# Key norms by one product with a block matrix of ones, and the steps of recurrence, inversion and finish in another order

## The chip, the cores and the metric

The kernel runs on one core of a Trainium2 chip, in one launch. The metric is the device time of one execution in microseconds (us). Six names recur: PE is TensorE (matrix products; its weight loads are shown apart as PEld), DVE is VectorE, ACT is ScalarE, POOL is GpSimd, SP is the engine that issues most transfers, and PSUM is the memory into which PE writes.

## The reference, cut to what matters

One hybrid decoder layer for 512 tokens of width 1024, in float32. A normalised stream feeds two mixers, RWKV-7 time mixing (16 heads of 64 channels) and a native sparse attention; their outputs are gated, merged, projected, and followed by a gated MLP with a short convolution. What the change touches is in the time mixing:

```python
r, k, v, wd, ad, gd = split_cols(z, RWKV_SPLIT)
decay = jnp.exp(-jnp.exp(w_log.astype(f32)))
a = jax.nn.sigmoid(a0 + ad @ a2)
g = jax.nn.sigmoid(gd) @ g2
kk = heads(k * k_k)
kk = kk / jnp.maximum(jnp.sqrt(jnp.sum(kk * kk, axis=-1, keepdims=True)), 1e-12)
k = k * (1.0 + (a - 1.0) * k_a)
# state = state * w + (state a) b^T + v k^T, token by token; y = state r
y = wkv7_scan(r_h, heads(decay), k_h, v_h, -kk, kk * a_h)
mean = jnp.mean(y, axis=-1, keepdims=True)
var = jnp.mean(jnp.square(y - mean), axis=-1, keepdims=True)
y = ((y - mean) * lax.rsqrt(var + GN_EPS)).reshape(B, S, RWKV_DIM)
y = y * ln_w + ln_b
y = (y + bonus.reshape(B, S, RWKV_DIM)) * g
```

and, at the end of the layer, `x = x + rms_norm(... @ ffn_down)`, whose sum of squares and root stand behind the last product.

## The kernel before, in words

**Wide products.** Each large weight matrix is cut in blocks of 128 columns. A block is split into a rounded part (named with h) by ScalarE and the rest (l) by GpSimd, and multiplied with the stream's parts in groups of three PE instructions of 128x512 (L306, L307, L308; the same three in other lines for the later projections). These triples are called wide products below; `k`, `r`, `v` (time mixing), `gt` (gates), `q`, `ksp`, `kwp` (attention) are their results.

**Who sets the order.** The program is written as generators. A function `drive(fill, ...)` goes in rounds: in each round every spawned generator advances by its own rate (0.6 steps, 1.05 steps, and so on, after a delay in rounds), and `fill`, a chain of projections, advances by one step, which is one triple. So a `yield` in a generator leaves room for a triple or two on PE at that place; more yields mean more wide products there, taken from the same chain. A scheduler then places the instructions on each engine's queue, mostly in the order in which they were written. Every engine works through its queue in order.

**Stages.** The 16 heads are 8 pairs (p = 0 to 7) in two groups (g = 0, 1) of four pairs (GP = 4). For each pair `prep` makes decays, key norms and scaled keys, and `couple` the products within chunks of 64 tokens, with the projections of the next pair as fill. For each group `invert` inverts 32x32 triangular blocks on DVE, `recur` joins them to 64x64 inverses on PE and then goes through 8 chunks of 64 tokens, and `finish` normalises the output and multiplies it with the output gate. In the run shown the first group's recurrence lies at 225 to 282 us, the second's at 437 to 488; then comes the attention's score stage (`pc` compressed scores, `s` scores of a head for 128 queries, `vtp`, `pt`, `pct` transposes, `o` values), with the rest of the query and key projections as fill, and from about 700 us the output projections and the MLP.

**The places the change touches.** Line numbers are those of the profile.

- `prep`. Q is the square of the scaled key, made by ACT. Four products `pn` (L541) of Q with `sel`, a 128x2 matrix that selects the two heads, give token norms in a 128x8 tile; ACT takes the root (L543, after a load of its table), DVE a maximum and a reciprocal (L544, L545), POOL spreads the result to 128x512 (L551, `nte`; ACT for pair 4), and four transposes (`pb`, L140 with `ident`) bring it back to channels by tokens. `EC` and `EN` are exponentials of the summed log decay `C` (a scan on DVE, L531) and its negative. `A` (L561, L562) needs `EN`, Q (L563) needs `EC`; `KB` (L570) and `AR` (L572) multiply with `pb`. `couple` multiplies `KB` and `AR` in the products `g` (L607).
- `recur`, joining: `mt` (L705) are 64 products of 32x32 per group in two halves (q) of two pairs (i); each half is evicted by ACT and DVE, then four yields, then `mm` (L728), 64 more, evicted into `TT` (L733 on ACT, L735 on DVE), then three yields.
- `recur`, the chunks: for chunk c, `xw` (L789) multiplies the state, DVE adds to W, 8 products with `TT` (L805) give U, which ACT and DVE evict into `UV` (L810 on ACT); a yield; `xs` (L815) are the products that renew the state; a yield. The output `y` is gathered in two PSUM banks for four chunks: `carried(c)` from the state (L753), `inner(c)` from `UV` (L760); every second chunk is copied to `YT` (L764). `inner(c - 1)` stands behind `xw` of chunk c.
- `finish`, for each pair: load and split of the gate weights (`gh` on ACT, `gl` on POOL; the copy at L854), load of the bonus `bvl`, transposes `gt`, scale and shift on ACT into `y2`, addition of `bvl` on POOL, the product `pg` (L880) and the multiplication on DVE (L881). `finish` of group 1 is spawned ahead of the scores at rate FN.
- `post`: at the end of each block of tokens ACT gives a sum of squares (L1361), DVE a product `p2tm` (L1363) and the total `p2ss` (L1364); ACT takes the root, DVE the reciprocal (L180) and two final steps (L1368).

## Time and profile before

| | |
|---|---|
| median of 3 runs | 1170.33 us (1169.43 to 1172.22) |
| the profiled execution | 1171.52 us |
| its span on the core | 1169.7 us |
| mean granted PE clock | 0.992 |
| instructions in the span | 19903 |
| DMA | 131.95 MB, mean 113 GB/s |

The span is the time from the first to the last instruction that the profiler saw; the execution's own time is 1.8 us more. A row of a timeline has start and duration; "xN" is a count of pieces that stand together (an fp32 product shows as two pieces), and in square brackets stands how long the engine had been idle and what released it. Since matmuls overlap, the durations of neighbours on PE add up to more than the time they take: the distance of starts is the time. A row of the waits has the engine and instruction that waited, who released it, the total, the number of times and the longest. A row of the windows has, for a stretch of time, the busy time and number of instructions of each engine, and the TensorE clock that was granted as a share of full speed.

### The profile page before, as it was taken

To read this page: it belongs to the slowest core of one execution; us is meant where nothing else is said; L and a number is where in the kernel's file an instruction comes from. 1 tells how busy PE (TensorE), PEld (TensorE's weight loads), DVE (VectorE), ACT (ScalarE), POOL (GpSimd) and SP (SyncE) were. 2 spreads that over 40 slices of the span, in tenths; PEclk is the share of its full clock that TensorE was granted. 3 is DMA by queue.
4 is the path that set the end of the run, shared out by engine and by line. 5 is a ranking of instruction groups with operands and counts; after the bars stand their busy time and mean duration, and the time that the engine had idled before them with its cause. 6 is when DMAs were issued, how large, how long until landed. Compare 5 with 4: busy or idle time off the path is not lost.

```text
span 1169.7 us, 19903 instructions
## 1 busy us (share of the span) xinstructions
PE 1148.6 (98%) x7418; PEld 927.3 (79%) x7418; DVE 574.0 (49%) x1196; ACT 579.5 (50%) x1149; POOL 595.2 (51%) x537
## 2 busy tenths in 40 slices
PE   9999999999999999999999999999999999999997
PEld 7888888867878887767677778889888888888886
DVE  4236555634456563587798735754443343331103
ACT  6446663534665334477576654534444444443311
POOL 4346654335666452497666635511565556554430
PEclk9999999989999999999999999999999999999999
DMA  7522335311443662225543136641233333334421
GB/s 245 134 65 75 103 99 167 96 64 53 113 125 93 188 198 92 91 60 145 170 149 97 46 97 181 209 156 39 80 99 99 97 94 99 99 97 136 127 64 72
DMA packets 95651, 131.95 MB, mean 113 GB/s; under 512 B 34177, under 2 KB 37057, under 8 KB 95298
## 3 DMA queue, kind: packets, MB, share of 16 engines
q1 hardware_dynamic: 79634, 116.26, 33.1%
q10 hardware_dynamic: 15920, 14.42, 3.9%
q8 instruction: 58, 0.95, 0.3%
q14 instruction: 39, 0.32, 0.1%
HBM read 108.30 MB, written 19.14 MB: 109 GB/s over the span
## 4 chain that ended last, share of the span: by engine, by line
PE 87%; DVE 4%; ACT 3%; POOL 2%; issue 1%; DMA 1%; SPq 0%; DVEq 0%; ACTq 0%; POOLq 0%
PE pu L223 6%; PE pu L221 6%; PE pu L222 6%; PE dn L1317 3%; PE dn L1316 3%; PE dn L1315 3%; PE o L1142 3%; PE pt L140 3%; PE ub L1199 3%; PE ub L1201 2%; PE ub L1200 2%; PE gt L306 2%; PE gt L308 2%; PE gt L307 2%; PE v L306 2%; PE v L308 2%
## 5 line engine op out<-in xcount | busy, mean ns | idle before, releaser
L1095 ACT ACTIVATE p<-p,stt 128x384 f32<-128x384 f32 (+3 forms) x128 | 70.7, 554 | 34.5 <-DVE stt L1093 32.9
L1069 POOL TENSOR_SCALAR p<-p,stt 128x512 f32<-128x512 f32 (+1 forms) x64 | 72.3, 1139 | 25.8 <-DVE stt L1064 15.5
L1457 DVE SCALAR_TENSOR_TENSOR u<-pu,cvec,u 128x511 f32<-128x511 f32 x44 | 33.0, 750 | 101.2 <-ACT u L1456 101.2
L1093 DVE CUSTOM_DVE_ANT_0 p<-s,rh 128x384 f32<-128x384 f32 (+3 forms) x128 | 59.0, 484 | 22.7 <-PE s L1079 18.3
L1463 DVE TENSOR_TENSOR al<-u,ah 128x512 fp32r<-128x512 f32 x22 | 23.8, 1080 | 45.4 <-ACT ah L1462 45.4
L140 PE MATMUL pt<-ident,p 128*128 128x128 f32 x320 | 44.3, 272 | 0.0
L1086 PE MATMUL s<-kst,qs 128*128 128x512 f32 (+1 forms) x128 | 39.2, 396 | 4.4 <-DVE stt L1093 4.1
L1461 POOL TENSOR_TENSOR u<-u,u 128x512 f32<-128x512 f32 x22 | 28.3, 1288 | 27.3 <-DVE u L1458 26.3
L1142 PE MATMUL o<-PT,vt 128*64 128x256 f32 (+3 forms) x256 | 41.5, 443 | 0.0
L140 PEld LDWEIGHTS pt<-ident,p 128*128 128x128 f32 x320 | 37.8, 141 | 4.4 <-issue 0.4
L1069 DVE TENSOR_SCALAR p<-p,stt 128x512 f32<-128x512 f32 (+1 forms) x64 | 35.3, 580 | 0.8
L1456 ACT ACTIVATE u<-pu,cvec 128x512 f32<-128x512 f32 x44 | 33.6, 764 | 3.0 <-PE pu L1419 3.0
L1458 DVE SCALAR_TENSOR_TENSOR u<-pu,cvec,u 128x510 f32<-128x510 f32 x44 | 33.0, 749 | 1.6
L1086 PEld LDWEIGHTS s<-kst,qs 128*128 128x128 f32 x128 | 20.9, 189 | 13.5 <-DVE stt L1093 9.3
L1142 PEld LDWEIGHTS o<-PT,vt 128*64 128x64 f32 x256 | 16.6, 136 | 18.8 <-issue 16.8
L1133 ACT ACTIVATE PT<-pt 128x512 f32<-128x512 f32 x48 | 27.3, 584 | 8.0 <-PE pt L140 7.8
L1363 DVE TENSOR_TENSOR p2tm<-dn,gb 128x512 f32<-128x512 f32 x4 | 2.8, 692 | 51.2 <-ACT p2jl L1361 51.2
L1135 DVE COPY PT<-pt 128x512 f32<-128x512 f32 x32 | 21.7, 678 | 8.4 <-PE pt L140 8.3
L1462 ACT ACTIVATE ah<-u 128x512 fp32r<-128x512 f32 x22 | 13.9, 633 | 22.0 <-POOL u L1461 22.0
L1095 ACT ACTIVATION_READ_ACCUMULATOR p<-p,stt 128x1 f32 x128 | 24.2, 189 | 0.0
L664 DVE TENSOR_TENSOR XP<-XP,TM 128x30 f32<-128x30 f32 (+14 forms) x60 | 20.3, 338 | 2.0
L162 POOL TENSOR_TENSOR up3l<-up30r,up3h 128x512 fp32r<-128x512 f32 x1 | 1.3, 1295 | 38.2 <-ACT up3h L124 38.2
(1755 smaller groups left out, 3953.8 us busy)
## 6 DMA issues: line engine op xcount, KB each, us to landing
gtd<-gt ACTq DMA_DIRECT2D x16, 256.0 KB, 2.2
qs<-qd SPq DMA_DIRECT2D x32, 128.0 KB, 3.3
g<-gtd SPq DMA_DIRECT2D x16, 256.0 KB, 3.2
xt<-in_x_dram SPq DMA_DIRECT2D x4, 512.0 KB, 5.5
bvd<-bv SPq DMA_DIRECT2D x8, 256.0 KB, 2.2
bvl<-bvd SPq DMA_DIRECT2D x8, 256.0 KB, 2.9
oad<-y SPq DMA_DIRECT2D x8, 256.0 KB, 2.5
kst<-kst ACTq DMA_DIRECT2D x16, 128.0 KB, 2.5
```

What stands on the lines that cost most here:

```text
L140: return te.transpose(o, i, ident)
L221: te.matmul(p, wh(k), mh(k), start=first and k == 0, stop=False)
L222: te.matmul(p, wh(k), ml(k), start=False, stop=False)
L223: te.matmul(p, wl(k), mh(k), start=False, stop=last and k == n - 1)
L306: te.matmul(p, wh(k), hh[:, k, :], start=k == 0, stop=False)
L308: te.matmul(p, wl(k), hh[:, k, :], start=False, stop=k == KT - 1)
L1069: (po if b else ve).tensor_scalar(o.pe[e, b, k], o.pe[e, b, k], st[e][:, 3, i:i + 1], None, op0=OP.mult)
L1086: m = te.matmul(s_[:, :n], qt, kt[:, x, b, :n], start=x == 0, stop=x == 1)
L1093: ve.tensor_tensor_reduce(sb, parts[b], rh[e][:, (3 - qb) * 128:], -1.0, BIG, OP.add, OP.min, st[e][:, 0, i:i + 1])
L1095: sc.activation(sb, sb, AF.Exp, scale=-1.0, bias=st[e][:, 0, i:i + 1], accum_out=st[e][:, 1, i:i + 1])
L1142: te.matmul(acc[e * 64:e * 64 + 64, j * 128:], vt[:, j, b * 256 + g * 64:b * 256 + g * 64 + 64], m[e][:, c:c + n], start=False, stop=k == ...
L1199: te.matmul(p, wh(k), sh[:, k, :], start=k == 0, stop=False)
```

## The change

1. **Key norms.** The 128x128 matrix `onesr`, with ones in the two 64x64 blocks of a head, multiplies Q in one fp32 product: `pb` in PSUM holds the sum of squares of the head in every one of its channels. DVE raises it to at least 1e-24, ACT takes the logarithm and then exp(-0.5 ...) in place. The factors 2 and -2 become 0.5 and -1, so the first use of `pb` becomes a scalar_tensor_tensor. `sel` goes.
2. **Joining the inverses.** After each quarter (q, i) of `mt` and of `mm` there are two yields; the four yields and the three yields behind them become one each.
3. **Chunks.** `inner(c)` stands at the end of its own chunk, behind `xs`; `carried(c)` is always ahead of W, for c = 4 too; the two `y` banks are taken when c is a multiple of 4.
4. **Finish.** The gate weights are loaded and split in place of a helper, with the rest part cut to what is used; the shift `lnb` goes into the DVE multiplication. In group 0 DVE adds the scaled transposes to `bvl` in place (no ACT step, no POOL addition; two `bvl` buffers in turn), in group 1 ACT scales and POOL adds as before, with one yield more. FN becomes 1.3.
5. **post.** `p2ss` stands ahead of `p2tm`.

The diff, without the constants `sel`:

```diff
--- before.py
+++ after.py
@@ -34,3 +34,3 @@
 PR, CR, IY, FR = 0.6, 0.5, 31, 0.5
-ID, IE, RD, RR, NG0, NQ1, PX, FN = (30, 30), (54, 54), (67, 67), (1.05, 0.85), 8, 4, 3, 1.15
+ID, IE, RD, RR, NG0, NQ1, PX, FN = (30, 30), (54, 54), (67, 67), (1.05, 0.85), 8, 4, 3, 1.3
 NW, NU, PA = 13, 3, 0.25
@@ -538,15 +537,7 @@
         yield
-        pn = (pz if p == GP else py)(f"pn{p}")
-        for t in range(4):
-            te.matmul(pn[:, 2 * t:2 * t + 2], Q[:, t * 128:(t + 1) * 128], sel, start=True, stop=True)
-        nt = rw.tile([128, 8], F32, tag="nt", name=f"nt{p}", bufs=2)
-        sc.activation(nt, pn[:, :8], AF.Sqrt)
-        ve.tensor_scalar(nt, nt, 1e-12, 2.0, op0=OP.max, op1=OP.mult)
-        ve.reciprocal(nt, nt)
-        nte = rw.tile([128, 8, 64], F32, tag="T", name=f"nte{p}", bufs=NT)
-        nb = nt[:, :, None].to_broadcast([128, 8, 64])
-        if p == GP:
-            sc.activation(nte, nb, AF.Copy)
-        else:
-            po.tensor_copy(nte, nb)
+        pb = pz(f"pb{p}")
+        te.matmul(pb, onesr.bitcast(F32), Q, start=True, stop=True)
+        ve.tensor_scalar(pb, pb, 1e-24, None, op0=OP.max)
+        sc.activation(pb, pb, AF.Ln)
+        sc.activation(pb, pb, AF.Exp, scale=-0.5)
         EC = rw.tile([128, 8, 65], F32, tag="EC", name=f"EC{p}", bufs=1)
@@ -566,8 +557,6 @@
         yield
-        pb = pz(f"pb{p}")
-        for t in range(4):
-            tr(pb[:, t * 128:(t + 1) * 128], nte[:, 2 * t:2 * t + 2].rearrange("p a b -> p (a b)"), ident)
-        ve.tensor_tensor(KB[:, :, 0, :], pb.rearrange(c8, t=64), A.rearrange(c8, t=64), op=OP.mult)
+        ve.scalar_tensor_tensor(KB[:, :, 0, :], pb.rearrange(c8, t=64), 0.5, A.rearrange(c8, t=64), op0=OP.mult,
+                                op1=OP.mult)
         o.Q = None if gr else Q
-        ve.scalar_tensor_tensor(gr.AR[p % GP][:, 0, :] if gr else Q, Q, -2.0, pb, op0=OP.mult, op1=OP.mult)
+        ve.scalar_tensor_tensor(gr.AR[p % GP][:, 0, :] if gr else Q, Q, -1.0, pb, op0=OP.mult, op1=OP.mult)
         tc.keep_in_program_order(ve.scalar_tensor_tensor(F, R, vec[:, V_RK + p:V_RK + p + 1], F, op0=OP.mult,
@@ -708,2 +697,4 @@
                             tc.keep_in_program_order(m)
+                yield
+                yield
             for h in range(2):
@@ -718,4 +709,3 @@
             behind(sc.activation(gr.diag[0][lo, :, 0:32], gr.diag[1][lo], AF.Copy))
-        for _ in range(4):
-            yield
+        yield
         for q in range(GP // 2):
@@ -729,2 +719,4 @@
                                   stop=True)
+                yield
+                yield
             for h in range(2):
@@ -736,7 +728,6 @@
         YT = gr.YT = rh_.tile([128, 4, GP, 2, 64], F32, tag="XB", name=f"YT{g}", bufs=2)
-        for _ in range(3):
-            yield
+        yield
         hs = [slice(0, 64), slice(64, 128)]
         iv = "p (i v) -> p i v"
-        yps = {}
+        yps = [None]
 
@@ -745,5 +736,5 @@
         def ybank(c):
-            if c // 4 not in yps:
-                yps[c // 4] = [py(f"y{g}{c}{h}").rearrange("p (a i v) -> p a i v", i=GP, v=64) for h in range(2)]
-            return [b[:, c // 2 % 2] for b in yps[c // 4]]
+            if c % 4 == 0:
+                yps[0] = [py(f"y{g}{c}{h}").rearrange("p (a i v) -> p a i v", i=GP, v=64) for h in range(2)]
+            return [b[:, c // 2 % 2] for b in yps[0]]
 
@@ -756,3 +747,3 @@
         def inner(c):
-            y = ybank(c)
+            y = ybank(c) if c == 0 else [b[:, c // 2 % 2] for b in yps[0]]
             for h in range(2):
@@ -790,3 +781,2 @@
                                   St[hs[h], i], start=True, stop=True)
-                inner(c - 1)
                 if c != 4:
@@ -823,5 +813,5 @@
                 St = SN
+            inner(c)
+            if c < 7:
                 yield
-            else:
-                inner(c)
         stat2(2, free)
@@ -851,7 +841,11 @@
             gh = rh_.tile([128, 256], F32R, tag="gh", name=f"gh{p}", bufs=1)
-            gl = rh_.tile([128, 256], F32R, tag="gl", name=f"gl{p}", bufs=1)
-            split_to(a["g2"][p], gh, gl, f"g2{p}", 256, p=rh_, late=True, tag="TM", bufs=1)
-            po.tensor_copy(gh[64:96, 128:], gl[64:96, 128:].bitcast(F32))
+            gl = rh_.tile([128, 128], F32R, tag="gl", name=f"gl{p}", bufs=1)
+            raw = rh_.tile([128, 256], F32, tag="TM", name=f"g2{p}r", bufs=1)
+            sy.dma_start(raw, a["g2"][p])
+            tc.keep_in_program_order(sc.activation(gh, raw, AF.Copy))
+            po.tensor_tensor(gl, raw[:, :128], gh[:, :128].bitcast(F32), op=OP.subtract)
+            gx = gh[64:96, 128:]
+            po.tensor_tensor(gx, raw[64:96, 128:], gx.bitcast(F32), op=OP.subtract)
             yield
-            bvl = rh_.tile([128, S], F32, tag="bvl", name=f"bvl{p}", bufs=1)
+            bvl = rh_.tile([128, S], F32, tag=("bvl", "TB")[g == 0 and i % 2], name=f"bvl{p}", bufs=1)
             tc.keep_in_program_order(sy.dma_start(bvl, bvd[p]))
@@ -862,3 +856,3 @@
                 tr(pt[:, t * 128:(t + 1) * 128], Y8[:, t].rearrange("p h v -> p (h v)"), ident)
-            y2 = rh_.tile([128, S], F32, tag="TB", name=f"y2{p}", bufs=1)
+            y2 = bvl if g == 0 else rh_.tile([128, S], F32, tag="TB", name=f"y2{p}", bufs=1)
             y2v = y2.rearrange("p (t s u) -> p t s u", s=2, u=64)
@@ -866,8 +860,9 @@
             lnw, lnb = vec[:, V_LNW + p:V_LNW + p + 1], vec[:, V_LNB + p:V_LNB + p + 1]
-            if i % 2 == 0:
-                sc.activation(y2, pt, AF.Identity, scale=lnw, bias=lnb)
-            else:
-                for x in range(2):
-                    sc.activation(y2v[:, :, x], ptv[:, :, 1 - x], AF.Identity, scale=lnw, bias=lnb)
-            po.tensor_tensor(y2, y2, bvl, op=OP.add)
+            for y_, p_ in ([(y2, pt)] if i % 2 == 0 else [(y2v[:, :, x], ptv[:, :, 1 - x]) for x in range(2)]):
+                if g:
+                    sc.activation(y_, p_, AF.Copy, scale=lnw)
+                else:
+                    ve.scalar_tensor_tensor(y_, p_, lnw, y_, op0=OP.mult, op1=OP.add)
+            if g:
+                po.tensor_tensor(y2, y2, bvl, op=OP.add)
             yield
@@ -875,2 +870,3 @@
                 yield
+                yield
             pg = px(f"pg{p}")
@@ -878,5 +874,5 @@
             te.matmul(pg, gh[:, :128], lg1l, start=False, stop=False)
-            te.matmul(pg, gl[:, :128], lg1h, start=False, stop=False)
+            te.matmul(pg, gl, lg1h, start=False, stop=False)
             te.matmul(pg, gh[:96, 128:], lg2, start=False, stop=True)
-            ve.tensor_tensor(y2, y2, pg, op=OP.mult)
+            ve.scalar_tensor_tensor(y2, y2, lnb, pg, op0=OP.add, op1=OP.mult)
             sy.dma_start(oad[p], y2)
@@ -1362,4 +1358,4 @@
         tm = p.tile([128, 512], F32, tag=name + "tm", name=f"{name}tm{t}", bufs=3)
-        ve.tensor_tensor(tm, acc, gb[:, 512:], op=OP.mult)
         ve.tensor_tensor(ss[:, 2:3], ss[:, 0:1], ss[:, 1:2], op=OP.add)
+        ve.tensor_tensor(tm, acc, gb[:, 512:], op=OP.mult)
         r = rstd_of(ss[:, 2:3], D, f"{name}r{t}", p)
```

What it does to the order on an engine, at three places. First PE at the start of the first group's joining (`gt`, L306 to L308, is fill); before:

```order
L308 MATMUL gt_2323<-hh,gt04l_2325 128x512
L541 MATMUL pn_2345<-sel,Q_2301 128x2 x4
L306 MATMUL gt_2323<-hh,gt04h_2324 128x512
L307 MATMUL gt_2323<-hl,gt04h_2324 128x512
L308 MATMUL gt_2323<-hh,gt04l_2325 128x512
L705 MATMUL mt_2365<-x_2126 32x32 x32
L705 MATMUL mt_2400<-x_2126 32x32 x32
L306 MATMUL gt_2323<-hh,gt04h_2330 128x512
```

and now (L694 is the line of `mt` in the changed kernel):

```order
L308 MATMUL gt_2277<-hh,gt04l_2279 128x512
L694 MATMUL mt_2313<-x_2080 32x32 x16
L306 MATMUL gt_2277<-hh,gt04h_2284 128x512
L307 MATMUL gt_2277<-hl,gt04h_2284 128x512
L308 MATMUL gt_2277<-hh,gt04l_2285 128x512
L306 MATMUL gt_2277<-hh,gt04h_2284 128x512
L307 MATMUL gt_2277<-hl,gt04h_2284 128x512
L308 MATMUL gt_2277<-hh,gt04l_2285 128x512
L694 MATMUL mt_2313<-x_2080 32x32 x16
L306 MATMUL gt_2277<-hh,gt04h_2284 128x512
```

A row of `mt` with x32 or x16 is that many products of 32x32. All 64 stood together, and `pn` of pair 4 stood three rows ahead; now there are four pieces of 16 with six wide products between them, and `pn` is gone. `mm` is cut in the same way. Counted over the first group's joining and chunks the wide products rise from 63 to 95 and the blocks of small products from 22 to 31; over the second's from 74 to 97 and from 23 to 32.

Second PE in the score stage, at the first head pairs (L1079 and L1086 before, L1075 and L1082 now, are `s`); before:

```order
L307 MATMUL ksp_5461<-hl,ksp1h_5462 128x512
L1079 MATMUL s_5442<-kst_4161,qs_4884 128x512 x2
L308 MATMUL ksp_5461<-hh,ksp1l_5463 128x512
L306 MATMUL ksp_5461<-hh,ksp1h_5462 128x512
L307 MATMUL ksp_5461<-hl,ksp1h_5462 128x512
L308 MATMUL ksp_5461<-hh,ksp1l_5463 128x512
L1079 MATMUL s_5484<-kst_4161,qs_4884 128x256 x2
L306 MATMUL ksp_5461<-hh,ksp1h_5462 128x512
L307 MATMUL ksp_5461<-hl,ksp1h_5462 128x512
```

and now:

```order
L1075 MATMUL s_5344<-kst_4063,qs_4667 128x512 x2
L1075 MATMUL s_5386<-kst_4063,qs_4667 128x256 x2
L140 MATMUL pt_5457<-ident,p_5265 128x128
L140 MATMUL pt_5457<-ident,p_5228 128x128
L140 MATMUL pt_5457<-ident,p_5268 128x128
L140 MATMUL pt_5457<-ident,p_5231 128x128
L140 MATMUL pct_5448<-ident,sc_5209 64x128
L1075 MATMUL s_5403<-kst_4063,qs_4670 128x512 x2
L140 MATMUL pct_5448<-ident,sc_5209 64x128 x2
L1075 MATMUL s_5422<-kst_4063,qs_4670 128x256 x2
```

The wide products `ksp` stood between the scores; now 16 of them stand inside the second recurrence, and at this place scores and transposes follow each other. Between the end of the second recurrence and the compressed scores `pc` of the next pair 31 wide products stood before, 8 do now; `kwp` products, which came later, now stand between that `pc` and that pair's scores.

Third ACT in `prep` of pair 1; before:

```order
L535 ACTIVATE pa_1158<-pa_1158,vd 128x512
L537 ACTIVATE F_1162<-pa_1158,vd 128x512
L543 ACT_TABLE_LOAD
L543 ACTIVATE nt_1175<-pn_1170 128x8
L555 ACT_TABLE_LOAD
L555 ACTIVATE EC_1181<-C_1153 128x8x64
L556 ACTIVATE EN_1182<-C_1153 128x512
L330 ACTIVATE K_1131<-k_1132,vd 128x512
```

and now (L541 is Ln, L542 Exp on `pb`, L546 `EC`, L547 `EN`):

```order
L534 ACTIVATE pa_1145<-pa_1145,vd 128x512
L124 ACTIVATE r2h_1206<-r21r 128x512
L536 ACTIVATE F_1149<-pa_1145,vd 128x512
L546 ACTIVATE EC_1162<-C_1140 128x8x64
L541 ACT_TABLE_LOAD
L541 ACTIVATE pb_1157<-pb_1157 128x512
L547 ACT_TABLE_LOAD
L547 ACTIVATE EN_1163<-C_1140 128x512
L542 ACTIVATE pb_1157<-pb_1157 128x512
```

`EC` has moved ahead of the first table load, `EN` behind the second. The number of table loads is the same over the whole kernel, 25.

More of the change, by code (lines that the diff above doesn't have):

```diff
@@ L326, in hybrid_layer @@
     rmask = rconst("rmask", [128, S])
-    sel = rconst("sel", [128, 2])
     def shift(p, o, mc, n=128):
@@ L1362, in post @@
         tm = p.tile([128, 512], F32, tag=name + "tm", name=f"{name}tm{t}", bufs=3)
+        ve.tensor_tensor(ss[:, 2:3], ss[:, 0:1], ss[:, 1:2], op=OP.add)
         ve.tensor_tensor(tm, acc, gb[:, 512:], op=OP.mult)
-        ve.tensor_tensor(ss[:, 2:3], ss[:, 0:1], ss[:, 1:2], op=OP.add)
         r = rstd_of(ss[:, 2:3], D, f"{name}r{t}", p)
@@ L1557, in layout @@
     d["onesb"] = (hb[:, None] == hb[None]).astype(f)
-    d["sel"] = (hb[:, None] == np.arange(2)[None]).astype(f)
     dist = np.arange(128)[:, None] + 384 - np.arange(512)[None]
```

## The prediction

> **What bounds the kernel now.** I read the page first: the span, then the busy shares.
>
> ```profile
> span 1169.7 us, 19903 instructions
> ```
>
> ```profile
> PE 1148.6 (98%) x7418; PEld 927.3 (79%) x7418; DVE 574.0 (49%) x1196; ACT 579.5 (50%) x1149; POOL 595.2 (51%) x537
> ```
>
> TensorE (PE) is busy for 98% of the span and every other engine for about half. So an edit counts if it shortens PE's in-order queue, lets PE run faster, or fills one of the 21 us in which PE stands. The profiled execution took 1171.52 us, 1.2 above the median of 1170.33; the sum below is made against the former and carried to the latter as a difference. Next I read stretches around PE's small products, and a stretch of the score stage behind the second recurrence (columns: stretch, length, busy time and count of PE, of its weight loads, VectorE, ScalarE, GpSimd, then granted clock, DMA share, GB/s).
>
> ```profile
> 222.00:229.40 7.40, 7.40 (x111) 6.36 (x111) 2.93 (x5) 4.86 (x8) 0.84 (x2) 1.00 0.21 74
> 229.40:233.20 3.80, 3.80 (x58) 3.25 (x53) 1.58 (x3) 3.70 (x6) 0.00 (x0) 0.55 0.02 4
> 240.30:247.10 6.80, 6.80 (x19) 4.12 (x20) 2.11 (x3) 1.25 (x3) 3.94 (x3) 0.52 0.38 118
> 441.30:445.20 3.90, 3.90 (x11) 3.07 (x11) 0.70 (x1) 3.86 (x3) 0.00 (x0) 0.56 0.02 6
> 488.10:505.30 17.20, 16.72 (x93) 13.39 (x92) 16.18 (x59) 13.53 (x43) 12.74 (x15) 1.00 0.28 93
> ```
>
> Rows 2 to 4: PE is busy without a gap, but at half clock. Row 5: VectorE is busy 16.18 of 17.20 us, so there PE is not the only bound. Third, what PE waits for between 80 and 1000 us (total, times, longest):
>
> ```profile
> PE s L1086 <- DVE stt L1093: 4.1, 7, 1.3
> PE xs L815 <- ACT UV L810: 2.3, 4, 0.8
> PE s L1079 <- DVE y L881: 1.3, 1, 1.3
> PE xs L805 <- DVE TT L735: 0.9, 1, 0.9
> PE pg L880 <- POOL gh L854: 0.9, 1, 0.9
> PE r L308 <- POOL r6l L162: 0.6, 1, 0.6
> PE xw L805 <- DVE TT L735: 0.4, 1, 0.4
> ```
>
> The waits that the edits touch are short, so the sum is one of small terms of both signs.
>
> **Key norms on PE (a).** PE around the two old pieces, for pair 0, from its timeline (start, duration):
>
> ```profile
> 83.39 0.95 PE L541 MATMUL pn<-sel,Q 128*128 128x2 f32 x8
> 84.21 0.48 PE L306 MATMUL k<-hh,k1h 128*128 128x512 f32 x1
> 84.53 0.40 PE L307 MATMUL k<-hl,k1h 128*128 128x512 f32 x1
> 84.76 0.39 PE L308 MATMUL k<-hh,k1l 128*128 128x512 f32 x1
> ```
>
> and, 2.3 us further on,
>
> ```profile
> 87.03 0.60 PE L140 MATMUL pb<-ident,nte 128*128 128x128 f32 x4
> 87.39 0.48 PE L306 MATMUL k<-hh,k1h 128*128 128x512 f32 x1
> ```
>
> Matmuls overlap, so a price is the distance of starts. A wide fp32r product costs 0.23 (84.53 to 84.76); the first one after other work costs 0.32, so leaving such work costs 0.09. `pn` costs 0.82 + 0.09, `pb` 0.36 + 0.09: together 1.36. Their replacement is one fp32 product of 128x128 by 128x512. The chain of waits has such a product at full clock, for another tile:
>
> ```profile
> 12.31 0.86 PE b L250 x2
> ```
>
> 0.86 + 0.09 = 0.95. So PE gains 0.41 in each of 8 pairs: **-3.3**.
>
> **Key norms on the other engines (b).** The scan on VectorE for the same pair, then ScalarE's rows behind it, then VectorE's first and last step towards `AR`, PE's product `g` that needs it, and last the place in pair 3 where PE stood for `AR`:
>
> ```profile
> 83.17 1.22 DVE L531 TENSOR_TENSOR_SCAN C<-rmask,T 128x512 f32<-128x512 f32 x1 [0.76 <-POOL T L530]
> ```
>
> ```profile
> 85.29 1.28 ACT L555 ACT_TABLE_LOAD   x1
> 86.59 0.63 ACT L555 ACTIVATE EC<-C 128x512 f32<-128x512 f32 x1
> 87.13 0.61 ACT L556 ACTIVATE EN<-C 128x512 f32<-128x512 f32 x1
> ```
>
> ```profile
> 87.92 0.68 DVE L561 SCALAR_TENSOR_TENSOR A<-pa,EN 128x512 f32<-128x512 f32 x1
> ```
>
> ```profile
> 91.46 0.67 DVE L572 SCALAR_TENSOR_TENSOR AR<-Q,pb 128x512 f32<-128x512 f32 x1
> ```
>
> ```profile
> 93.02 1.16 PE L607 MATMUL g<-AR,KB 64*128 64x128 f32 x16
> ```
>
> ```profile
> 166.60 1.61 PE L607 MATMUL g<-AR,KB 64*128 64x128 f32 x24 [0.16 <-DVE AR L572]
> ```
>
> In ScalarE's new order `EC` follows the scan (83.17 + 1.22 = 84.39), then come a table load, Ln, a second load, `EN`, and the last Exp. With `EC` taking 0.54 from start to start, loads of 1.28, and Ln and Exp in PSUM like this row of a tanh in PSUM,
>
> ```profile
> L535 ACT ACTIVATE pa<-pa,vd 128x512 f32<-128x512 f32 x8 | 5.2, 652 | 0.0
> ```
>
> `EN` starts near 84.39 + 0.54 + 1.28 + 0.65 + 1.28 = 88.1, 1.0 later than 87.13. VectorE's `A` waits for it; `Q`, which only needs `EC`, moves ahead of it, so `A` and all behind it come 0.9 later, and the product `g` is queued on PE behind `AR`. The slack is 93.02 - (91.46 + 0.67) = 0.9: this just uses it up. The removed GpSimd copy and two tiny VectorE steps are off the path now; the new VectorE maximum runs while ScalarE loads a table. But in pair 3 PE already stands 0.16 for `AR`, and there the new order puts no more wide products ahead of `g` than before (36 and 36 from `pa`; 39 instead of 37 in pairs 1, 2, 5 and 6). I take 0.2 of wait in those four pairs, 0.8 in pairs 3 and 7, none in 0, whose slack is the one shown, and none in 4, which is prepared inside the first recurrence, long ahead of its `g`: **+2.4**. Bounds: 0 (the slack covers all), 1.25 in each of 8 pairs, about one table load, = 10.
>
> **The inversion tail (c, d).** The 64 small products `mt` of a group (128 pieces in the trace) stand in a row, with this after them:
>
> ```profile
> 227.04 3.80 PE L705 MATMUL mt<-x 32*32 32x32 f32 x128
> 230.77 0.79 PE L306 MATMUL gt<-hh,gt04h 128*128 128x512 f32 x1
> ```
>
> PE was busy for 7.40 of 7.40 us before 229.40, and yet the clock then fell to 0.55: I read it as the answer to a stretch of products that use little of the array. `mt` keeps its pace in slow stretches (as many pieces per us behind 229.40 as ahead of it), so only wide products pay: from 230.77 to 233.20 2.43 x 0.45 = 1.1, then 6.80 x 0.48 = 3.3, in group 1 3.90 x 0.44 = 1.7. The change cuts each row into four chunks (3.73 / 4 = 0.93 us) with six wide products (6 x 0.23 = 1.4 us) between. I take it that the clock stays up: **-6.1**; the other end is 0. The waits of `xs` and `xw` for the VectorE eviction of `TT` (0.9 + 0.4) get wide products ahead of them: **-1.3** (0 if these are too few).
>
> The Trainium skill, "TensorE: Matmul & The Clock Gate", Part 1 and "Why this matters for your kernels", lets the clock drop after a window of some 3.4 us in which PE idles. By that rule alone the mixing, which removes no such gap, gains nothing: (c) is 0 and the sum +3.45. The 222.00 to 229.40 row disagrees: no idle time, and the clock drops. So the rule of the Trainium skill gets a rival of low chance, not the sum.
>
> **What the mixing costs (e).** Each change from wide to small products and back costs PE:
>
> ```profile
> 251.19 0.40 PE L308 MATMUL gt<-hh,gt14l 128*128 128x512 f32 x1
> 251.51 0.69 PE L815 MATMUL xs<-UV,BKT 128*64 128x64 f32 x16
> 252.13 0.50 PE L306 MATMUL gt<-hh,gt14h 128*128 128x512 f32 x1
> 252.47 0.39 PE L307 MATMUL gt<-hl,gt14h 128*128 128x512 f32 x1
> ```
>
> 0.32 instead of 0.23 going in, 0.34 instead of 0.23 coming out: 0.20. Blocks of small products between wide ones rise from 22 to 31 in the first recurrence and from 23 to 32 in the second: 18 x 0.20 = **+3.6** (half if the exit alone counts: 1.8).
>
> **Fillers used up early (f).** The second recurrence takes 23 more wide products (74 to 97). They came from the score stage: 31 stood there before the next pair's compressed scores `pc`, 8 do now. Moved work costs PE nothing, if the stage left behind shrinks by 23 x 0.228 = 5.2. It can't wholly: VectorE had 16.18 of 17.20, so it gives back about 1.0; and `ksp`/`kwp` products that now stand before the next pair's `s` cover some of the wait of `s` for VectorE (4.1 in all), say 0.8. 5.2 - 1.0 - 0.8 = **+3.4** (0 to 5.2). The first group's 32 moved fillers leave a stage where PE is the bound and cost nothing.
>
> **Recurrence and finish (g, i).** `inner(c)`, 8 small products, moves from behind the next `xw` to directly behind `xs`; it covers the eviction of the state that a wide product covered. Only the first product into the second pair of `y` banks is new in its wait, for the copies of `YT`: +0.2 (0 to 0.7). In `finish`, GpSimd loses one subtract of half width, a copy for a subtract, and for group 0 an addition of 128x512 that moves to VectorE's existing step; the waits of `pg` for `gh` (0.9) and of `r` for `r6l` (0.6), both on GpSimd's queue near that work, may go: -1.2 of 1.5. Together **-1.0**. ScalarE loses group 0's Identity, VectorE gains it as a step that reads PSUM; at half load each in that stage this is hidden. Group 1's `finish`, with one yield more per pair at rate 1.3 for 1.15, I leave at 0, with 1.3 either way (the `s` that waits for its `y`).
>
> **The tail (h).** After the last product nothing covers anything:
>
> ```profile
> 1163.94 0.69 DVE L1363 TENSOR_TENSOR p2tm<-dn,gb 128x512 f32<-128x512 f32 x1 [2.70 <-ACT p2jl L1361]
> 1164.55 0.15 DVE L1364 TENSOR_TENSOR p2ss<-p2ss 128x1 f32<-128x1 f32 x1
> 1164.73 0.30 ACT L124 ACTIVATE p2r<-p2ss,vec 128x1 f32<-128x1 f32 x1 [0.82 <-DVE p2ss L1364]
> 1165.06 0.16 DVE L180 RECIPROCAL p2r<-p2r 128x1 f32<-128x1 f32 x1 [0.36 <-ACT p2r L124]
> ```
>
> `p2ss` now goes at 1163.94, the root at 1164.12, ready at 1164.45; the reciprocal queues behind `p2tm`, to about 1164.7: **-0.35** (-0.6 if VectorE gets free sooner, -0.2).
>
> **Sum.** -3.3 + 2.4 - 6.1 - 1.3 + 3.6 + 3.4 - 1.0 - 0.35 = -2.65: the profiled 1171.5 becomes 1168.9, and the median 1170.33 becomes **1167.7**. A measurement of this kernel tells 0.2%, 2.3 us, from no change (the three runs lie 2.8 apart); so 1168.0 is the border of faster.
>
> **Rivals.** *Clean gain*: fillers leave without loss (f = 0) and the longer key-norm chain stays inside its 0.9 of slack (b = 0): -2.65 - 3.4 - 2.4 = -8.45, 1161.9. For it: 39 instead of 37 wide products ahead of `g`; against it: VectorE's 16.18 of 17.20. *Gains given back*: f at 5.2, b at 4: -2.65 + 1.8 + 1.6 = +0.75, 1171.1; for it the same row 5. *The key-norm chain stalls PE (slower)*: two table loads and two long activations now stand in one row on ScalarE, with pair work and weight splits queued on it; if `g` waits 1.25 in every pair, b is 10 and the sum -2.65 + 7.6 = +4.95, 1175.3. It decides from +2.3, so b = 7.35 or 0.92 a pair; against it is the 0.9 of slack shown. *The clock drops all the same*: as many small products remain, and low use may be reckoned over a stretch longer than one row of `mt`; then c = 0, +3.45, 1173.8. The idle rule of the Trainium skill, cited above, would end at the same time.
>
> **How the numbers follow.** Forecast 0.42, clean gain 0.18, given back 0.20, stall 0.12, clock 0.08. The forecast's own range is 1165 to 1170.5, of which 0.30 lies below the border and 0.12 within. Faster 0.30 + 0.18 = 0.48; within 0.2% 0.12 + 0.18 = 0.30; slower 0.12 + 0.08 + 0.02 = 0.22. The range reaches from just below the clean gain to 1173, between given back and the two slower cases; outside are about half of clean gain's spread and most of the stall and the clock, 0.2.
>
> **What will show it.** (c) right: a granted clock near 1.00 all through `mt` and `mm`; wrong: a stretch at 0.5 to 0.6. (b): the waits of `g` for `AR`, 1 to 4 us in all; over 7 means the stall. (a): the `pb` product at 0.86 with a distance of 0.95 to the second wide product. (e): the number of 0.50-long first wide products. (f): idle time of PE in the 20 us after the second recurrence, 3 to 5 us where it was 0.5; below 1 means clean gain. (g): no `pg` wait for `gh`. (h): the reciprocal 1.1 after the last `p2jl` instead of 1.35. The prediction is wrong if `xs` waits for `UV` (2.3 now) grow with ScalarE's new order, which I left as it is.

## The result, and the profile after

The changed kernel is slower: 1177.68 us median of four runs (1174.27, 1177.66, 1177.69, 1177.79) against 1170.18 before, a ratio of 1.0054 with a 95% interval of 1.004 to 1.0067. (The ratio weighs all executions; the medians alone give 1.0064.) Forecast was 1167.7, with a range from just below 1161.9 to 1173. The profile is of the 1174.27 execution. From its page, the span and the busy times:

```profile
span 1172.5 us, 19714 instructions
...
PE 1142.6 (97%) x7338; PEld 916.5 (78%) x7338; DVE 585.8 (50%) x1194; ACT 581.8 (50%) x1150; POOL 577.0 (49%) x526
```

PE has 6 us less to do and takes 2.8 us longer over it, so its idle time grew by 9. What it waits for between 80 and 1000 us (total, times, longest):

```profile
PE g L596 <- DVE AR L561: 8.2, 6, 2.2
PE s L1082 <- DVE stt L1089: 4.5, 6, 1.6
PE pt L140 <- POOL p L1065: 2.0, 2, 1.3
PE pct L140 <- POOL sc L1041: 2.0, 1, 2.0
PE pg L873 <- DVE stt L1089: 1.2, 1, 1.2
```

The first row is the rival "the key-norm chain stalls PE": `g` waited 0.3 us in all before and 8.2 now, 0.9 to 1.1 in four pairs and 2.2 in pairs 3 and 7. The second row is little changed (4.1 before); the three below it are new waits, in the score stage. Now the stretches, in the columns used before: PE's wait in pair 3, what follows it, `mt` and `mm` of the two groups, and the score stage.

```profile
166.40:168.60 2.20, 0.03 (x1) 0.00 (x1) 2.09 (x4) 0.71 (x2) 1.81 (x2) 0.96 0.36 115
168.60:172.00 3.40, 3.37 (x32) 3.40 (x32) 2.52 (x4) 1.23 (x2) 1.05 (x1) 0.52 0.49 152
230.50:249.00 18.50, 18.50 (x303) 14.08 (x303) 9.24 (x12) 13.51 (x17) 6.60 (x5) 1.00 0.26 72
432.90:452.00 19.10, 19.10 (x306) 14.57 (x305) 3.47 (x5) 9.60 (x11) 5.86 (x5) 1.00 0.46 144
487.20:575.00 87.80, 75.64 (x410) 53.61 (x411) 64.93 (x215) 58.51 (x162) 61.21 (x68) 0.98 0.31 96
```

Rows 3 and 4 are what the forecast hoped for: both joinings run at full clock. Row 2 is what it did not see: behind the 2.2 us in which PE stood, the clock is at 0.52. Row 5 answers to this one of the kernel before:

```profile
488.10:575.00 86.90, 81.39 (x457) 59.83 (x457) 71.45 (x227) 62.95 (x171) 67.08 (x73) 1.00 0.36 105
```

Both windows end at 575. The second is 0.9 us longer and holds 47 fewer matmuls and 5.8 us less PE work. Put together, from the start of one PE instruction in both traces to the next:

| up to | before | after | change of the stretch |
|---|---|---|---|
| first `kc` product | 31.39 | 32.22 | +0.8 |
| first `mt` of group 0 (pairs 0 to 3) | 227.04 | 230.50 | +2.6 |
| first `pv` of pair 4 (joining and chunks of group 0) | 290.27 | 285.62 | -8.1 |
| first `mt` of group 1 (pairs 4 to 7, finish of group 0) | 437.33 | 432.91 | +0.2 |
| first `pc` of pair 0 (joining and chunks of group 1) | 488.07 | 487.10 | +3.5 |
| first `q7` (score stage) | 579.66 | 583.14 | +4.5 |
| end of the span | 1169.7 | 1172.5 | -0.7 |

The sum is the +2.8 of the spans. The +3.5 is with 23 more wide products, worth 5.2; the +4.5 is with 23 fewer. (Wherever wide products are counted or priced, here and in the forecast, one is a single PE instruction of 128x512, a third of a triple.)

### The profile page after: what moved, and what is told of

Read it like the earlier page. It is cut to its first block, busy times and chain, and to the rows that moved or that the text cites. A ratio compares the mean times of both kernels' runs of the same rounds, so it can differ in the third digit from the quotient of the medians.

```text
span 1172.5 us, 19714 instructions
## 1 busy us (share of the span) xinstructions
PE 1142.6 (97%) x7338; PEld 916.5 (78%) x7338; DVE 585.8 (50%) x1194; ACT 581.8 (50%) x1150; POOL 577.0 (49%) x526
## 4 chain that ended last, share of the span: by engine, by line
PE 87%; DVE 5%; ACT 3%; POOL 3%; issue 2%; DMA 0%; SPq 0%; ACTq 0%; DVEq 0%; POOLq 0%
PE pu L223 6%; PE pu L221 6%; PE pu L222 6%; PE dn L1313 3%; PE dn L1312 3%; PE dn L1311 3%; PE pt L140 3%; PE o L1138 3%; PE ub L1195 2%; PE ub L1197 2%; PE ub L1196 2%; PE gt L306 2%; PE gt L307 2%; PE gt L308 2%; PE v L307 2%; PE v L306 2%
## 5 line engine op out<-in xcount | busy, mean ns | idle before, releaser
L1089 DVE CUSTOM_DVE_ANT_0 p<-s,rh 128x384 f32<-128x384 f32 (+3 forms) x128 | 59.2, 484 | 28.2 <-PE s L1075 20.0
L1138 PE MATMUL o<-PT,vt 128*64 128x384 f32 (+3 forms) x256 | 43.0, 447 | 0.0
L1082 PE MATMUL s<-kst,qs 128*128 128x512 f32 (+1 forms) x128 | 38.2, 390 | 4.7 <-DVE stt L1089 4.5
L1454 DVE SCALAR_TENSOR_TENSOR u<-pu,cvec,u 128x510 f32<-128x510 f32 x44 | 32.9, 749 | 1.6
L1082 PEld LDWEIGHTS s<-kst,qs 128*128 128x128 f32 x128 | 21.5, 189 | 12.6 <-DVE stt L1089 8.6
L596 PE MATMUL g<-AR,KB 64*128 64x128 f32 x256 | 18.0, 294 | 8.2 <-DVE AR L561 8.2
L596 PEld LDWEIGHTS g<-AR,KB 64*128 64x128 f32 x256 | 16.6, 204 | 10.4 <-POOL ll L162 3.9
```

The costliest lines, as they stand in the source:

```text
L1082: m = te.matmul(s_[:, :n], qt, kt[:, x, b, :n], start=x == 0, stop=x == 1)
L1089: ve.tensor_tensor_reduce(sb, parts[b], rh[e][:, (3 - qb) * 128:], -1.0, BIG, OP.add, OP.min, st[e][:, 0, i:i + 1])
L1138: te.matmul(acc[e * 64:e * 64 + 64, j * 128:], vt[:, j, b * 256 + g * 64:b * 256 + g * 64 + 64], m[e][:, c:c + n], start=False, stop=k == ...
```

## The experiments

Ratios are against the kernel before, run beside each. An interval reaches 0.1 to 0.15% to either side, so two rows that differ by less than about 0.2% can't be told apart.

| kernel | ratio | 95% interval | median us |
|---|---|---|---|
| the change | 1.0054 | 1.004 to 1.0067 | 1177.68 |
| e1: the change with the old key norms | 1.0027 | 1.0013 to 1.0041 | 1172.65 |
| e2: the change, Ln and Exp behind EN | 0.9988 | 0.9975 to 1.0002 | 1168.13 |
| e3: the change, new yields in group 0 alone | 1.0009 | 0.9999 to 1.0019 | 1171.88 |
| e4: the change, old rate of finish | 1.0032 | 1.002 to 1.0044 | 1174.51 |
| e5: before + joining of group 0 | 0.997 | 0.9957 to 0.9983 | 1166.64 |
| e6: before + joining of both groups | 1.0043 | 1.0029 to 1.0057 | 1174.59 |
| e7: e2 + one yield per chunk in group 1 | 0.9917 | 0.9902 to 0.9931 | 1160.26 |
| e8: e7 + old rate of finish | 0.9885 | 0.987 to 0.99 | 1156.26 |
| e9: before + key norms | 1.0005 | 0.9994 to 1.0017 | 1172.33 |
| e10: before + key norms, Ln and Exp behind EN | 0.9957 | 0.9942 to 0.9972 | 1165.33 |
| e11: e8 + an empty place for `sel` | 0.9881 | 0.9865 to 0.9896 | 1156.57 |
| e12: e8 with the old key norms | 0.9918 | 0.9902 to 0.9933 | 1161.56 |

### What stalls `g`: the key norms or their order

Theory: the changed order on ScalarE puts `EN` behind two table loads, `A`, `KB` and `AR` on VectorE come late, and PE stands at `g`. Its rows in pair 3 of the changed kernel, from ScalarE's timeline, two of VectorE's, and PE's:

```profile
158.39 0.63 ACT L124 ACTIVATE gt10h<-gt101r 128x512 fp32r<-128x512 f32 x1 [1.08 <-POOL T L529]
158.92 0.76 ACT L536 ACTIVATE F<-pa,vd 128x512 f32<-128x512 f32 x1
159.59 0.62 ACT L546 ACTIVATE EC<-C 128x512 f32<-128x512 f32 x1
160.22 1.28 ACT L541 ACT_TABLE_LOAD   x1
161.52 0.58 ACT L541 ACTIVATE pb<-pb 128x512 f32<-128x512 f32 x1
162.12 1.28 ACT L547 ACT_TABLE_LOAD   x1
163.41 0.63 ACT L547 ACTIVATE EN<-C 128x512 f32<-128x512 f32 x1
163.95 0.58 ACT L542 ACTIVATE pb<-pb 128x512 f32<-128x512 f32 x1
```

```profile
164.08 0.69 DVE L552 SCALAR_TENSOR_TENSOR A<-pa,EN 128x512 f32<-128x512 f32 x1 [1.09 <-ACT EN L547]
...
167.80 0.68 DVE L561 SCALAR_TENSOR_TENSOR AR<-Q,pb 128x512 f32<-128x512 f32 x1
```

```profile
168.63 3.57 PE L596 MATMUL g<-AR,KB 64*128 64x128 f32 x32 [2.20 <-DVE AR L561]
```

VectorE stands 1.09 us for `EN` although `EC` needed no load (none stands between it and the tanh before). The Trainium skill ("ScalarE: Activation LUTs", "Table sets: the hidden batching unit") has a table set that serves logarithm and exponential with one load; the trace shows a load of 1.28 ahead of each, so it was not used here. e1 is the changed kernel with `prep` as it was before:

```diff
-        pb = pz(f"pb{p}")
-        te.matmul(pb, onesr.bitcast(F32), Q, start=True, stop=True)
-        ve.tensor_scalar(pb, pb, 1e-24, None, op0=OP.max)
-        sc.activation(pb, pb, AF.Ln)
-        sc.activation(pb, pb, AF.Exp, scale=-0.5)
+        (pn, nt, nte and the transposes of before, and sel)
```

> The changed kernel with part 1 undone (four pn products, root, reciprocal, spread, four transposes). Theory (the later EN stalls PE at g): the six waits of g for AR (8.2 us) and the stretch at clock 0.56 behind the one in pair 3 (1.5 us) go, and PE pays the old products again, about 0.65 us in each of 8 pairs as pair 0 shows (+5.2): -4.5 us against the changed kernel's profile, 1169.8. Rival (the waits of g come from where the new order put g, not from the key norms): waits of g stay near 8, time +5.

Measured: 1.0027, so 0.27% (3.2 us) less than the change, near the 4.5 expected; `g` waits 1.3 us in all, and there is no stretch at half clock in pair 3. The waits belong to the key norms. e2 keeps the new norms and moves two lines:

```diff
         te.matmul(pb, onesr.bitcast(F32), Q, start=True, stop=True)
         ve.tensor_scalar(pb, pb, 1e-24, None, op0=OP.max)
-        sc.activation(pb, pb, AF.Ln)
-        sc.activation(pb, pb, AF.Exp, scale=-0.5)
...
         sc.activation(EN, C, AF.Exp, scale=-1.0)
+        sc.activation(pb, pb, AF.Ln)
+        sc.activation(pb, pb, AF.Exp, scale=-0.5)
```

> The changed kernel with Ln and Exp on pb written behind EN on ScalarE, so that EC and EN need no table load between them. Theory (A and what follows on VectorE waited for EN, which stood behind two table loads): waits of g for AR fall from 8.2 to below 1.5 us, no stretch at half clock in pair 3, -8 us, 1166 in the profile. Rival (pb itself is what comes too late, since its Ln, load and Exp end at the same time as before): waits of g stay at 6 to 9 us, time unchanged within 2 us.

ScalarE in pair 3 of e2, and its waits of `g`:

```profile
160.34 0.62 ACT L544 ACTIVATE EC<-C 128x512 f32<-128x512 f32 x1
160.86 0.62 ACT L545 ACTIVATE EN<-C 128x512 f32<-128x512 f32 x1
161.50 1.28 ACT L546 ACT_TABLE_LOAD   x1
162.79 0.58 ACT L546 ACTIVATE pb<-pb 128x512 f32<-128x512 f32 x1
```

```profile
PE g L596 <- DVE AR L561: 3.1, 5, 0.9
```

Measured: 0.9988, 0.66% (7.7 us) less than the change, where 8 was expected. `EN` starts 0.5 behind `EC` instead of 3.8, and 8.2 us of waits became 3.1; the expected "below 1.5" was missed. What is left is mostly PE's own gain: counted from the start of the scan, `AR` starts only 0.2 us later than in the kernel before (pairs 1, 2, 3, 6 and 7), and PE is ready for `g` 0.5 us sooner in pairs 3 and 7 and 0.9 in 1, 2 and 6. The 0.2 lies in VectorE's list, where the maximum (0.70) is new. The trace of e2 is of the longest of its ten executions (1173.84): its score stage has 17 us at half clock (495.6 to 505.8 and 522.9 to 529.7), so it is used here for the key norms alone.

Alone on the kernel before, the two versions of the key norms come out like this.

> The kernel before with the key norms of the change alone. Theory (EN behind two table loads): about 8 us of waits of g for AR, a stretch at half clock at pair 3 in some executions, 5 us of PE time saved, 0.8 lost in the first 32 us: 4 to 6 us slower than before, 1175. Rival (the waits need the change's other parts too): waits below 2 us and 3 us faster.

> The kernel before with the key norms of the change, Ln and Exp behind EN. Theory: waits of g 3 us, no half clock there; 5.2 saved, 0.8 lost at the start: 1 to 2 us faster than before, 1168.6. Rival (the new norms lose even so): 1 us or more slower.

e9 is 1.0005 (0.9994 to 1.0017): no change, where +5 was expected. `g` waits 7.7 us and half clock follows at pairs 3 and 7, so the mechanism is there, but the trade was reckoned too dark: from `mt` of group 0 to the last `y` e9 and e10 take 50.2 us and before 55.0, with as many wide products. In the first joining e9 has one half-clock stretch of 3.4 us, at 234, where before had one at 229.8 and another of 6.8 at 240.1. Before, pair 4's transposes stood there among the small products; that these made the difference is likely, not shown. e10 is 0.9957, 5 us faster, more than the 1 to 2 expected, with 3.1 us of waits and the same gain in the first joining. In the best kernel, whose joining has no half clock to lose, the norms are worth nearly as much:

> The kernel with one yield per chunk and the old finish rate, with the old key norms (and sel). Theory (with Ln and Exp behind EN the new norms gain): waits of g at 1 us, 5 us more PE work, 0.8 less at the start: 2 to 3 us slower, 1158.6. Rival (their PE time was hidden): the same or faster, 1156 or less.

e12 is 0.9918, 0.33% (3.9 us) above e8. So the product with the ones matrix gains, once its two activations stand behind the ones that PE waits for.

### What empties the score stage

The new yields draw 23 wide products into the second recurrence. Theory: the score stage needed them as fillers. Rival: the new rate of `finish` of group 1 makes the waits.

```diff
-                yield
-                yield
+                if g == 0:
+                    yield
+                    yield
```

in both places of e3, with the four and three yields back for group 1, and in e4:

```diff
-..., NG0, NQ1, PX, FN = ..., 8, 4, 3, 1.3
+..., NG0, NQ1, PX, FN = ..., 8, 4, 3, 1.15
...
             if g:
-                yield
                 yield
```

> The changed kernel with the new yields in the joining of group 0 alone; group 1's joining as before, so 34 wide products stand again between the second recurrence and the next pair's compressed scores, not 8. Theory (the score stage lost its fillers): PE's waits from 488 to 575 us fall from 11.8 to about 5, and the whole is 4 us faster than the changed kernel, although the slow stretch behind group 1's mt is back. Rival (finish of group 1, its rate and yields, makes these waits): they stay at 10 or more, and the time is 1 to 2 us longer.

> The changed kernel with finish of group 1 at the rate 1.15 and without the extra yield. Theory of e3 (fillers): waits of PE from 488 to 575 us within 2 us of 11.8, time within 2 us. Rival (finish of group 1): these waits fall to about 5 us and the time by 5.

e3: 1.0009, 0.45% less than the change; waits from 487 to 575 us fall from 11.8 to 8.0, not 5, with a new one, in e3's view of the waits:

```profile
PE kwp L308 <- POOL kwp1l L162: 3.0, 1, 3.0
```

PE waits for a weight split on GpSimd, which is behind four steps of `finish` (4.07 us, at 505.44) in its queue. e4: 1.0032, 0.22% less than the change, and waits of 9.7. So neither theory has it all. e5 and e6 take the question to the kernel before, where `finish` is as it was: the yields in group 0 (`if g == 0:` as in e3), and in both.

> The kernel before with one thing of the change: the joining of group 0 cut into chunks with yields (group 1's joining, key norms, recurrence and finish as before). Theory (the first recurrence's gain of 8 us comes from the joining: no slow stretch, no wait for TT, against some switches of kind): no stretch at half clock near 229 and 240 us, waits of xs and xw for TT gone, 4 to 6 us faster than before, 1165. Rival (the gain comes from the new order of inner and carried): less than 2 us faster.

> The kernel before with the joining of both groups cut into chunks. Theory (in group 1 the yields draw 23 wide products out of the score stage): PE's waits from 488 to 575 us rise from 5.0 to 10 or more, and it is 3 to 6 us slower than the kernel with group 0's joining alone, about as before. Rival (the score stage only suffers together with the new finish): another 1.5 us faster than with group 0 alone.

Windows of e5 (the first joining, and the half-clock stretch behind `mt` of group 1), and of e6 (the second joining, the score stage, and a stretch in it):

```profile
227.00:247.00 20.00, 20.00 (x310) 15.10 (x310) 8.05 (x14) 13.54 (x19) 6.81 (x5) 1.00 0.26 80
435.50:439.10 3.60, 3.60 (x38) 2.95 (x34) 1.10 (x2) 2.67 (x3) 0.00 (x0) 0.53 0.13 47
```

```profile
432.50:452.00 19.50, 19.50 (x307) 14.91 (x307) 3.47 (x5) 9.96 (x12) 6.26 (x5) 1.00 0.52 155
486.80:575.00 88.20, 78.07 (x420) 55.34 (x421) 69.22 (x221) 60.97 (x166) 63.27 (x70) 0.98 0.31 95
499.50:502.90 3.40, 3.26 (x14) 2.44 (x14) 3.06 (x12) 1.92 (x8) 3.32 (x3) 0.50 0.20 77
```

e5 is 0.997, 3.3 us faster than before: the joining of group 0 gains, a little less than the 4 to 6 expected (its profiled execution is 4.9 us shorter). e6 is 1.0043: group 1's joining in the same manner costs 0.73%, 8 us, more than expected, although it takes a half-clock stretch away. In the traces, from `mt` of group 1 to the last `y` it takes 50.5 us in e5 and 54.3 in e6 (23 more wide products), and from there to `q7` 91.6 and 95.0 with 23 fewer. The half clock in the last row of e6 costs little: its stretch, the first of the table, takes 16.0 us with it, and 15.8 in e4, which has none there. The time from one pair's `pc` to the next shows where the loss is:

| from `pc` of pair | before | e5 | e6 | change | e4 | e7 | e8 |
|---|---|---|---|---|---|---|---|
| 0 to 1 | 17.2 | 17.2 | 16.0 | 15.8 | 15.8 | 16.8 | 16.8 |
| 1 to 2 | 29.9 | 29.9 | 33.3 | 32.9 | 33.2 | 28.9 | 30.1 |
| 2 to 3 | 25.7 | 25.8 | 26.9 | 28.2 | 26.2 | 29.9 | 25.6 |
| 3 to 4 | 27.7 | 27.8 | 27.8 | 28.1 | 26.6 | 26.9 | 26.6 |

The stretch that lost its fillers (the wide products between the score work) shrinks from e5 to e6 by 1.3 us, about the 1.0 that the forecast had read from VectorE's 16.18 of 17.20. The one behind it, with as many wide products as before (27), grows by 3.4, and the third by 1.2. That PE, having run ahead, met the same VectorE and GpSimd work one stretch later fits with its waits there (5.6 us for 2.9), but no run took that work away, so it is argued, not shown. The changed rate of `finish` costs on top, in the third and fourth stretch (the change against e4).

### Both losses undone

e7 is e2 with one yield per chunk in group 1's joining (the diff, in both places), and none behind `mt`, so that the second recurrence takes 76 wide products; e8 has the old rate of `finish` and one yield less in it as well.

```diff
                 yield
-                yield
+                if g == 0:
+                    yield
```

> The changed kernel with Ln and Exp behind EN, and with one yield instead of two in each chunk of group 1's joining and none behind it, so that the second recurrence takes 76 wide products (before 74, changed 97) and 29 are left to the score stage. Theory (both losses undone, clock kept in both joinings): waits of g about 3 us, of the score stage 5 to 7, no half clock near mt or mm; 1163. Rival (the score stage's loss is not of fillers): waits there above 10, 1168.

> As the kernel with one yield per chunk, and finish of group 1 at rate 1.15 without its extra yield. Theory: within 1.5 us of that kernel. Rival (finish of group 1 holds the scores up): 3 us faster.

e7 is 0.9917; e8 is 0.9885, 13.6 us faster than before, with the first rows of its page and its windows of both joinings and of the score stage:

```profile
span 1154.4 us, 19724 instructions
...
PE 1137.3 (99%) x7338; PEld 914.2 (79%) x7338; DVE 588.3 (51%) x1194; ACT 582.2 (50%) x1150; POOL 578.7 (50%) x526
```

```profile
226.40:246.00 19.60, 19.60 (x308) 14.96 (x308) 9.78 (x13) 14.50 (x18) 6.57 (x5) 1.00 0.29 87
425.90:444.00 18.10, 18.10 (x340) 13.46 (x340) 4.65 (x8) 9.69 (x12) 4.71 (x4) 1.00 0.36 113
475.00:565.00 90.00, 85.07 (x485) 63.14 (x484) 73.92 (x235) 64.49 (x177) 70.68 (x76) 1.00 0.39 113
```

One yield is enough for the clock in group 1, and the score stage has its fillers. That e8 lies 0.32% (3.7 us) below e7 speaks for the rival there: the rate and the extra yield cost 3 to 4 us by themselves, in the third stretch of the table (29.9 against 25.6). There PE waits 2.8 us for ScalarE ahead of a `pt` in e7, and 3.4 us at half clock follow; e8 has neither.

### Where the longer executions differ

The profiled execution of the change was the shortest of four, so 3.4 us of its loss were not in that trace. Two more traces of the same kernel were taken.

> The changed kernel once more, for another trace: its executions came at 1174.3 and at 1177.7. Theory (the longer ones have more stretches at half clock, whose windows of 3.4 us lie elsewhere against the program): an execution near 1177.7 shows one or two more of them in the score stage or at a g, and the same waits. Rival (a wait, a transfer that lands later): the same stretches, and a new wait of 2 us or more.

> As the run before it: the changed kernel, another trace, the same two expectations.

They took 1175.82 and 1177.49 us. In both the waits are the same, and a second stretch at half clock stands behind the 2.2 us wait of pair 7; windows of the second of them, before and in it:

```profile
373.80:375.60 1.80, 0.32 (x5) 0.35 (x7) 1.75 (x3) 0.00 (x0) 1.06 (x1) 1.00 0.46 146
375.60:379.00 3.40, 3.40 (x33) 3.18 (x30) 2.32 (x5) 1.23 (x2) 1.18 (x2) 0.50 0.43 154
```

It costs 1.5 us there (in the first trace the products `g` of pair 7 took 2.06, here 3.51). The other 1.7 of the 3.2 lie in the first 13 us, where the first product `n1p` starts at 8.99 instead of 8.01 and the ones behind it later still. So one half of the gap is the clock, as expected, and the other the start, which no expectation had; why the start differs stays open.

## Why the prediction was wrong

**(b) failed: the key-norm chain.** Forecast +2.4 of waits, bounds 0 and 10. Measured: 8.2 of waits, and 1.5 for each half-clock stretch that a 2.2 us wait brings, one or two of them: 9.7 to 11.2, the rival to which 0.12 was given. The step that failed is the place of `EN` and the slack, both read from pair 0 and taken for all pairs. In pair 0 of the changed kernel both exponentials stand ahead of the loads:

```profile
85.26 0.63 ACT L546 ACTIVATE EC<-C 128x512 f32<-128x512 f32 x1 [0.65 <-DVE C L530]
85.80 0.62 ACT L547 ACTIVATE EN<-C 128x512 f32<-128x512 f32 x1
...
87.06 1.28 ACT L541 ACT_TABLE_LOAD   x1
```

In pair 4 it is the same, and these two pairs do not wait. In pairs 1, 2, 3, 6 and 7 the order is that of pair 3 shown above, and `EN` comes 1.9 us later than before, not 1.0 (1.3 in pair 5). Pair 3 of the kernel before, for comparison:

```profile
157.01 1.23 DVE L531 TENSOR_TENSOR_SCAN C<-rmask,T 128x512 f32<-128x512 f32 x1 [0.76 <-POOL T L530]
160.97 0.61 ACT L556 ACTIVATE EN<-C 128x512 f32<-128x512 f32 x1
165.87 0.68 DVE L572 SCALAR_TENSOR_TENSOR AR<-Q,pb 128x512 f32<-128x512 f32 x1
```

In the change the scan of pair 3 starts at 157.50. Counted from it, `EN` starts at 5.9 for 4.0 and `AR` at 10.3 for 8.9, 1.4 later. From `EC` to `EN` pass 3.82, as priced (3.75); but `EC` itself starts at 2.1 and not at 1.2, right behind the scan, since a weight split (`gt10h`, 158.39, after 1.08 of waiting) and `F` stand ahead of it on ScalarE. PE for its part is ready for `g` 0.5 us sooner than before in pairs 3 and 7, and 0.2 in 1, 2 and 6: the gain of (a) is taken from the same stretch of PE that covered the chain. So pairs 1, 2, 5 and 6 wait 0.9 to 1.1, and 3 and 7, which had no slack, 2.2.

**(f) failed: the fillers.** Forecast +3.4 for both stretches, at most 5.2. e6 against e5 gives about 8 for the yields in group 1; with the half-clock stretch that they save (1.7) and their switches (1.8 by the forecast's price), the loss is again about 8. The first stretch gave back what was foreseen; a bound that stops at "the moved work costs its own time" left out that the stage behind can get longer: the next stretch grew by 3.4.

**Group 1's finish** was left at 0 with 1.3 either way; e4 (2.6 us, hardly more than the runs can tell apart) and e8 against e7 (3.7 us) show that it cost about 3. Together (b), (f) and this are some 15 us above the forecast, of which the median of the change (10 us above it) shows what is left after the gains below.

**(c) and (d) held.** Both joinings run at 1.00, the waits of `xs` and `xw` for `TT` are gone. The rule of the Trainium skill ("TensorE: Matmul & The Clock Gate", Part 1: the clock drops after a window of idle time) did not govern these places: before, it dropped with PE 7.40 of 7.40 busy, and the mixing cured that. But it does describe the new ones: behind 2.2 us with PE busy for 0.03 the clock is at 0.52, behind waits of 0.95 in e2 it stays at 1.00. The rule's 3.4 us of idle time were not needed. The rival drawn from it priced the joinings, where the rule did not hold, and not `g`, where it nearly does.

**(a) was better than forecast.** PE around the new product in pair 0:

```profile
84.17 1.02 PE L539 MATMUL pb<-Q,onesr 128*128 128x512 f32 x2
84.63 0.80 PE L306 MATMUL k<-hh,k1h 128*128 128x512 f32 x1
85.27 0.40 PE L307 MATMUL k<-hl,k1h 128*128 128x512 f32 x1
```

From 84.17 to 85.27 pass 1.10, less the wide product's 0.23 that is 0.87 and not 0.95: 0.49 gained for 0.41. The whole gain is larger: from `pv` of pair 1 to that of pair 2 pass 24.61 before, and 24.83 in the change, of which 0.90 is the wait of `g`. So PE saves 0.68 a pair, about 5.4 in 8 by this pair; that the rest lies in fewer changes between kinds of products is an estimate.

**(e), (g), (h), (i).** (g) held: no `pg` wait for `gh`, no `r` wait for `r6l`. (i): PE waits 0.2 for `YT` once, as said; but the new order of `inner` and `carried` brought a gain that the forecast had left out and feared as a loss. The waits of `xs` for `UV`, 2.3 before, are gone in the change, in e1 and in e12, all with the new order; in e5, without it, they are 2.5. From `mt` of group 0 to the last `y` e12 takes 54.9 us and e5 57.6, with 95 and 94 wide products between. (h) held, by this:

```profile
1167.31 0.16 DVE L1359 TENSOR_TENSOR p2ss<-p2ss 128x1 f32<-128x1 f32 x1 [3.16 <-ACT p2jl L1357]
1167.39 0.68 DVE L1360 TENSOR_TENSOR p2tm<-dn,gb 128x512 f32<-128x512 f32 x1
1167.50 0.30 ACT L124 ACTIVATE p2r<-p2ss,vec 128x1 f32<-128x1 f32 x1 [0.23 <-DVE p2ss L1359]
1167.99 0.15 DVE L180 RECIPROCAL p2r<-p2r 128x1 f32<-128x1 f32 x1
```

From `p2ss` ahead of `p2tm` to the reciprocal 0.68 pass; before, from `p2tm` to it, 1.12 (1163.94 to 1165.06): 0.44 gained for 0.35. (e) alone was not measured: e5 has it together with (c) and (d), and from `mt` of group 0 to the last `y` takes 57.6 us for before's 55.0, with 31 more wide products of 7.1; 4.5 gained for the forecast's 1.1 + 3.3 + 1.3 - 1.8 = 3.9.

## What to carry to other kernels

A gain on the busiest engine shortens the cover of every chain that ran beside it, so take the slack of a longer chain after that gain, and from each of its repetitions, not from the first: here the first had its instructions in another order than most. Where yields or priorities move fillers, ask what the stage they leave waits for, over several of its rounds: here 23 moved products cost 8 us, though their own time is 5.2. And a change that loses as a whole can hold a gain that a few lines set free: key norms behind `EN`, one yield less in group 1 and the old rate make it 1.2% faster than before.
